# A held load, column sums moved forward and feed-forward casts put in order, in a one-core hybrid encoder layer

## The chip, the core and the metric

The kernel runs on one core of a Trainium2 chip. A core has a matrix engine (TensorE, PE in the profile, with its weight loads shown apart as PEld), a vector engine (DVE), a scalar engine (ACT), GpSimd (POOL) and SyncE (SP). Each takes its own instructions in the order in which they stand in its program. Transfers from memory are issued by SP, ACT or POOL. The metric is the time of one execution on the device in microseconds, taken as the median of several runs.

## What is computed

One layer of a streaming encoder on x (512 rows of 1024) with 256 memory rows of 1024, everything float32:

```python
u = rmsnorm(h, g_mix)
gq, gk, gv, gg, ga, fq, fk, fv, ff, mq, gates = split_cols(u @ w_in, PROJ_SIZES)
...
mk, mv = split(rmsnorm(mem, g_mem) @ w_mem_kv)
...
merged = gt[0] * y_gla + gt[1] * y_fox + gt[2] * y_mem
h = h + merged @ w_out
u2 = rmsnorm(h, g_ffn)
h = h + square(relu(u2 @ w_ff1)) @ w_ff2
return rmsnorm(h, g_final)
```

`rmsnorm` divides each row by the root of its mean square and multiplies by a gain. The three branches (gated linear attention, forgetting attention, attention into the memory rows) lie between the first projection and `merged`; the change does not touch them.

## The kernel before

A float32 product is made of three products of rounded halves: every operand is split into a high part (`hi`, a copy rounded to fp32r, mostly by ACT) and a low part (`lo`, the operand minus its high part, by DVE), and PE forms high by high, high by low and low by high. So each weight of 128x1024 values (512 KB) costs a load, one cast on ACT and one subtraction on DVE before PE can use it. Weights lie in memory as numbered chunks (`wst`). The pool `wp` has three slots each for raw weights, for `hi` and for `lo`, taken in turn: a cast waits until PE has read the weight that held its slot.

PE's program order is the order of the code. The other engines' order is set by a planner that simulates the kernel at build time, except where it is written by hand: `in_order` chains all DVE, ACT and SP instructions traced inside it in the order of the code, and `tc.issue_after(ins)` (also as `behind(ins)`) puts the instructions of its block behind `ins` if they run on the same engine as `ins`. Neither adds a wait between engines. `tc.add_manual_dep(..., Sync, ...)` does: the instruction waits until the other has ended.

The front goes so. Ten matmuls on zeros (L302) keep PE busy until data are there. The memory rows come in four pairs (`mem_load`), each 128 partitions of two times 256 values; the first carries 24 columns of gains behind it. Pairs 0 and 1 go through ACT's queue, pairs 2 and 3 through SP's. For each of eight k, ACT multiplies the rows by their gain (`mxh`, L321) and DVE makes the low part (`mxl`, L323). `lead` loads the chunks 0 to 3 (weights of the memory keys), each split in two halves by ACT (L286) and DVE (L288); chunk 0 is loaded in two halves. `mem_keys` multiplies them (L391, twelve matmuls for each k).

Chunks 4 to 7 are the weights of the memory values. `mem_values` is a generator of 16 pieces, four for each chunk: for two row tiles the products with `hi` (four matmuls each), then for both those with `lo` (two each), at L404. Chunks 4 and 5 come through `lead`, chunks 6 and 7 (the third and the fourth) into `vraws`, whose tiles are those of chunks 3 and 4, and are split by `lead_w` (L416, L417).

x arrives in quarters (`x_load`, L339). `x_square` (L344) squares each on ACT; DVE adds the squares up (`x_sum`, L350) into `ssum`. Behind x on SP stand chunk 6 (L360), the identity (L361), chunk 7 (L362), the query and key weights of the forgetting attention and a small weight `g_raw` (all L153), then constants. Column sums (L430, eight matmuls of one column) give the row sums of squares; DVE scales them (L431), POOL takes the power (L432), and four transposes with the identity spread the result over all partitions (L437). Then for each of eight k: DVE scales x (L441), ACT makes `uhi` (L444), DVE makes `ulo` (L447). Inside that loop, behind the second `uhi`, ACT casts the small weight into `gw` (L457), a `hi` slot that chunk 7 held. PE begins the first projections with `uhi` and `ulo` as they come (`first_pair`, L609, L521, L522, L618), with the last two pieces of `mem_values` in between; when these end, ACT copies their results out (L407, `gqT`).

Much later, `w_out` is multiplied in two halves of 512 columns by `gN`, four chunks each. In the first half the chunks come one after the other, 24 PE steps each, through `get_w` (slots of `wp`). In the second half (`c1`) all four are asked for at once: the first two through `own_w` into tiles of their own (`f0`, `f1`; split at L223 and L224), the last two through `get_w`, hence `split_w` (L160, L161). A row tile then takes 24 steps: six for each chunk. When 24 units of `c1` have been issued (three row tiles), the first two feed-forward weights (`f2`, `f3`) are asked for with `own_w`. Their casts and subtractions are placed by the planner. `split_w` remembers its cast and subtraction in `cast_now` and `low_now`. The feed-forward part that follows works in four quarters of the inner width.

Of the kernel before, what the change touches and what calls it, by code (L numbers as in the profile page):

```python
# [13 lines left out]
AF = mybir.ActivationFunctionType  # L14
ALU = mybir.AluOpType
AX = mybir.AxisListType

P = 128
# [45 lines left out]
def hybrid_block(ctx, tc, chunks, wst, memT, xT, xN, gffn, gfin, wup, cst, out):  # L64
# [201 lines left out]
    with pool("front") as fp:  # L266
# [6 lines left out]

        def lead(key, loads=1, parts=1, after=(None, None, None)):

# [3 lines left out]
            for i in range(loads):  # L279
                sl = slice(i * 1024 // loads, (i + 1) * 1024 // loads)  # L280
                with behind(after[0]):
                    d = nc.sync.dma_start(raw[:, sl], wst[index[key]][:, sl]).ins
            for i in range(parts):
                sl = slice(i * 1024 // parts, (i + 1) * 1024 // parts)
                with behind(after[1]):
                    a = nc.scalar.copy(hi[:, sl], raw[:, sl]).ins  # L286
                with behind(after[2]):
                    v = nc.vector.tensor_tensor(lo[:, sl], raw[:, sl], f(hi[:, sl]), op=ALU.subtract).ins  # L288
                after = yield d, a, v
# [11 lines left out]
        for _ in range(10):  # L301
            nc.tensor.matmul(ps, wz[:, :P], wz, start=True, stop=True)  # L302
        def mem_load(eng, j, end=0, after=None):
            n = 2 * M
            at = j and j * P * n + P * 24
            with behind(after):
                return eng.dma_start(mem_s[:, (3 - j) * n:(4 - j) * n + end],
                                     memT[at:at + P * (n + end)].rearrange("(p c) -> p c", p=P)).ins

        mem_load(nc.scalar, 0, 24)  # L310
        d = mem_load(nc.scalar, 1)
        with tc.issue_after(d):
            act = nc.scalar.activation(warm, warm, AF.Exp).ins
        vec, load = None, None
        for j in range(4):
            parts = None
            if j > 1:
                load = mem_load(nc.sync, j, after=load)
            for k in (2 * j, 2 * j + 1):
                with behind(act):  # L320
                    act = nc.scalar.mul(mxh[:, k, :], memr[:, KT - 1 - k, :], gmem[:, k:k + 1]).ins  # L321
                with behind(vec):
                    vec = nc.vector.scalar_tensor_tensor(mxl[:, k, :], memr[:, KT - 1 - k, :], gmem[:, k:k + 1], f(mxh[:, k, :]),  # L323
                                                         op0=ALU.mult, op1=ALU.subtract).ins
                if parts is None:
                    parts = lead(chunks[j], 1 if j else 2, 2, (load, act, vec))
                    load, act, vec = next(parts)
# [7 lines left out]
        next(lead(chunks[4], after=(load, act, vec)))  # L335
        sqs = []

# [3 lines left out]
        def x_square(j):  # L341
            sq = fp.tile([P, 2, S], F32, tag="xsq", name=nm("xsq"), bufs=3)
            for k in range(2) if j == 3 else [slice(0, 2)]:
                nc.scalar.activation(sq[:, k], xt[:, 2 * j:2 * j + 2, :][:, k], AF.Square)  # L344
            if j == 1:
# [13 lines left out]
        vraws = [fp.tile([P, 1024], F32, tag="lead", name=nm("raw"), bufs=2) for _ in range(2)]  # L359
        nc.sync.dma_start(vraws[0], wst[6])  # L360
        nc.sync.dma_start(ident, cst[:, :P])  # L361
# [63 lines left out]
        lead_w(chunks[6], vraws[0])()  # L425
        run(islice(mv, 9))
        lead_w(chunks[7], vraws[1])()
        ps = at_()
        for t in range(NT):
            nc.tensor.matmul(ps[:, t:t + 1], ssum[:, t * P:(t + 1) * P], ones[:, 0:1], start=True, stop=True)  # L430
        nc.vector.tensor_scalar(ms, ps[:, :NT], 1.0 / D, EPS, op0=ALU.mult, op1=ALU.add)  # L431
        nc.gpsimd.tensor_tensor(rx, ms, mhalf[:, :NT], op=ALU.pow)  # L432
        k_copies(range(4))
        run(islice(mv, 3))
        rb = at_()
# [29 lines left out]
        u_low(KT - 1)  # L465
        run(islice(mv, 2))
        for j in range(4):
# [562 lines left out]
    with pool("outp") as op_:  # L1030
# [219 lines left out]
        run(islice(c1, 24))  # L1250
        ws = [own_w(("F", 0, 0, b)) for b in ("11", "21")]

# [614 lines left out]
def layout(inputs):  # L1867
# [48 lines left out]
    pairs = [tl(mem)[:, 2 * j:2 * j + 2][:, ::-1].reshape(P, -1) for j in range(4)]  # L1916
    mem_flat = np.concatenate([np.concatenate([pairs[0], cols], axis=1).ravel()] + [x.ravel() for x in pairs[1:]])
    wup = np.zeros((P, 264), np.float32)
# [47 lines left out]
```

## Time and profile before

| | us |
|---|---|
| median of 3 runs | 810.16 |
| lowest, highest run | 809.69, 810.54 |
| the profiled execution | 811.06 |
| its span, first to last instruction | 809.3 |

Times inside a profile count from the start of its span. A line of the timeline has the start, the duration, the engine, the line of the program, the operation, what it writes and reads, the shape and how often; in brackets stands how long the engine was idle before it and what ended this. A line of waits has the engine and what it did, whom it waited for, the sum, the number and the longest. A line of the stretches has the stretch, its length, the busy time of PE, PEld, DVE, ACT and POOL with their instructions, the granted clock, the share of the transfer engines and GB/s. In this execution the granted clock of PE was 0.997 of full speed.

### The profile page before, as it was taken

What the parts mean: (1) busy time and instruction counts of PE and PEld (TensorE: products, weight loads), DVE (VectorE), ACT (ScalarE), POOL (GpSimd) and SP (SyncE); (2) the same over time, 40 slices, a digit from 0 to 9 for tenths busy, and PEclk for the clock granted to TensorE, in tenths of its full rate; (3) what the DMA queues carried; (4) which work ended last, traced back from release to release, by engine and by line L of the source; (5) the groups of instructions that cost most, each with busy time, mean ns of one, the idle gap of its engine ahead of it and who ended that gap; (6) DMA issues with size and microseconds to landing.
All of it is one profiled execution on the core that took longest, in us unless ns stands there. A gap on an engine that the chain in (4) does not pass through costs nothing.

```text
span 809.3 us, 12486 instructions
## 1 busy us (share of the span) xinstructions
PE 800.1 (99%) x4799; PEld 704.9 (87%) x4799; DVE 595.6 (74%) x917; ACT 444.7 (55%) x702; POOL 108.0 (13%) x136
## 2 busy tenths in 40 slices
PE   9999999999999999999999999999999999999996
PEld 7788888888888888999999879988998899889985
DVE  6878878456465677877567368897788778877897
ACT  7767555443344234444354347874676367647764
POOL 0001010101101111143144000011001100100011
PEclk9999999999999999999999999999999999999998
DMA  9355665788887867757758723898758966896544
GB/s 358 137 160 175 185 164 178 213 226 246 215 266 239 234 210 198 186 138 206 204 134 238 254 81 130 275 258 217 240 165 195 220 213 173 191 274 202 162 83 130
DMA packets 39628, 161.29 MB, mean 199 GB/s; under 512 B 4752, under 2 KB 5456, under 8 KB 37200
## 3 DMA queue, kind: packets, MB, share of 16 engines
q0 software_dynamic: 9776, 58.20, 34.3%
q1 hardware_dynamic: 28432, 98.34, 34.2%
q10 hardware_dynamic: 1360, 3.96, 1.5%
q8 instruction: 37, 0.61, 0.3%
q14 instruction: 23, 0.19, 0.1%
HBM read 158.35 MB, written 35.68 MB: 240 GB/s over the span
## 4 chain that ended last, share of the span: by engine, by line
PE 94%; DMA 2%; DVE 1%; ACT 1%; issue 0%; POOLq 0%; DVEq 0%; POOL 0%; ACTq 0%
PE mm L1272 20%; PE mm L170 16%; PE mm L171 16%; PE mm L172 16%; PE a L171 5%; PE a L170 5%; PE a L172 5%; DMA raw<-in_wst_dram 2%; PE mm L391 1%; PE a L404 1%; PE a L662 1%; PE a L700 1%; PE a L699 1%; PE a L302 1%; PE a L939 1%; PE mm L618 0%
## 5 line engine op out<-in xcount | busy, mean ns | idle before, releaser
L170 PE MATMUL mm<-uhi,whi 128*128 128x512 f32 (+1 forms) x336 | 119.7, 356 | 0.0
L161 DVE TENSOR_TENSOR wlo<-raw,whi 128x1024 fp32r<-128x1024 f32 x61 | 79.6, 1306 | 53.0 <-ACT whi L160 53.0
L172 PE MATMUL mm<-uhi,wlo 128*128 128x512 f32 (+1 forms) x336 | 117.5, 350 | 0.0
L171 PE MATMUL mm<-ulo,whi 128*128 128x512 f32 (+1 forms) x336 | 117.3, 349 | 0.0
L160 ACT CAST whi<-raw 128x1024 fp32r<-128x1024 f32 x61 | 64.1, 1052 | 84.2 <-PE mm L171 47.8
L1328 ACT CAST hi<-raw 128x1024 fp32r<-128x1024 f32 x52 | 54.4, 1049 | 41.1 <-PE mm L1272 29.5
L1330 DVE TENSOR_TENSOR lo<-raw,hi 128x1024 fp32r<-128x1024 f32 x52 | 63.4, 1223 | 15.7 <-ACT hi L1328 15.7
L170 PEld LDWEIGHTS mm<-uhi,whi 128*128 128x128 f32 x336 | 63.7, 190 | 9.3 <-issue 1.5
L172 PEld LDWEIGHTS mm<-uhi,wlo 128*128 128x128 f32 x336 | 63.6, 189 | 8.5
L171 PEld LDWEIGHTS mm<-ulo,whi 128*128 128x128 f32 x336 | 63.7, 190 | 7.5
L1272 PE MATMUL mm<-u2l,hi 128*128 128x256 f32 x240 | 66.1, 283 | 0.0
L1272 PE MATMUL mm<-u2h,hi 128*128 128x256 f32 x240 | 66.1, 283 | 0.0
L1272 PE MATMUL mm<-u2h,lo 128*128 128x256 f32 x240 | 61.1, 283 | 0.0
L1632 POOL DMA_DIRECT2D b<-in_wst_dram x30 | 25.6, 855 | 262.2 <-DVE lo L1330 136.0
L1272 PE MATMUL mm<-u2sh,hi 128*128 128x256 f32 x192 | 52.5, 283 | 0.0
L1272 PE MATMUL mm<-u2sl,hi 128*128 128x256 f32 x192 | 52.5, 283 | 0.0
L170 PE MATMUL mm<-hi,ch 128*128 128x512 f32 (+1 forms) x132 | 50.9, 386 | 0.0
L171 PE MATMUL mm<-lo,ch 128*128 128x512 f32 (+1 forms) x132 | 50.9, 386 | 0.0
L172 PE MATMUL mm<-hi,cl 128*128 128x512 f32 (+1 forms) x132 | 50.9, 386 | 0.0
L1272 PE MATMUL mm<-u2sh,lo 128*128 128x256 f32 x192 | 47.5, 283 | 0.0
L1272 PEld LDWEIGHTS mm<-u2h,hi 128*128 128x128 f32 x240 | 46.1, 192 | 0.1
L1272 PEld LDWEIGHTS mm<-u2l,hi 128*128 128x128 f32 x240 | 46.1, 192 | 0.1
(446 smaller groups left out, 2144.9 us busy)
## 6 DMA issues: line engine op xcount, KB each, us to landing
raw<-in_wst_dram SPq DMA_DIRECT2D x113, 512.0 KB
raw<-T SPq DMA_DIRECT2D x32, 512.0 KB
b<-in_wst_dram POOLq DMA_DIRECT2D x32, 512.0 KB, 5.5
T<-in_wst_dram POOLq DMA_DIRECT2D x12, 1024.0 KB, 9.0
b<-in_wst_dram SPq DMA_DIRECT2D x16, 512.0 KB
wb<-in_wst_dram POOLq DMA_DIRECT2D x15, 512.0 KB, 5.4
T<-in_wst_dram POOLq DMA_DIRECT2D x12, 512.0 KB, 6.0
wb<-in_wst_dram SPq DMA_DIRECT2D x8, 512.0 KB
```

The costliest lines, as they stand in the source:

```text
L160: cast = nc.scalar.copy(hi, raw)
L161: low_now[0] = nc.vector.tensor_tensor(lo, raw, f(hi), op=ALU.subtract).ins
L170: nc.tensor.matmul(ps, lh, rh, start=start, stop=False, skip_group_check=on)
L171: nc.tensor.matmul(ps, lh, rl, start=False, stop=False, skip_group_check=on)
L172: nc.tensor.matmul(ps, ll, rh, start=False, stop=stop, skip_group_check=on)
L302: nc.tensor.matmul(ps, wz[:, :P], wz, start=True, stop=True)
L391: nc.tensor.matmul(kps[h], w[:, h * P:(h + 1) * P], x[:, k, :], start=k == p == 0, stop=k == KT - 1 and p == 2)
L404: nc.tensor.matmul(ps, x[:, k, sl], w[low][:, kk, :], start=k == low == 0 and x is mxh, stop=k == KT - 1 and low == 1)
L1272: nc.tensor.matmul(ps[:, a, :], x[:, a, k, :], y[:, s, k, :], start=start, stop=stop, skip_group_check=go is not None)
L1328: nc.scalar.copy(hi, raw)
L1330: nc.vector.tensor_tensor(lo, raw, f(hi), op=ALU.subtract)
L1632: nc.gpsimd.dma_start(to[i], wst[index["B", q, i, x]], accum_op=ALU.add)
```

## The change

There are four edits.

The start: the first pair of memory rows is loaded in two pieces on ACT's queue, with the gains in the first, and pair 1 moves to SP's queue, between the first and the second weight chunk. The high part of the first half of chunk 0 is made by DVE with a copy (`head=True`), ahead of DVE's first `mxl`, not by ACT.

The held load: the load of chunk 6 waits, as a dependency between engines, for the square of x's second quarter (`squares[1]`).

The column sums: they stand behind six pieces of `mem_values` instead of nine. Four pieces (before: three) come between them and the transposes, four (before: two) behind the transposes, and two are left for `first_pair` as before. So the sums stand three pieces and the transposes two pieces further forward. The low part of chunk 7 is traced behind the power and waits for it.

The feed-forward weights: the casts and subtractions of `f2` and `f3` are put behind the cast and the subtraction of the last chunk of `w_out`.

```diff
--- before.py
+++ after.py
@@ -271,7 +271,7 @@
         xt = fp.tile([P, KT, S], F32, name="xt")
         pre = {}
 
-        def lead(key, loads=1, parts=1, after=(None, None, None)):
+        def lead(key, loads=1, parts=1, after=(None, None, None), head=False):
 
             late = index[key] in (3, 4)
             raw = (fp if late else wp).tile([P, 1024], F32, tag="lead" if late else "raw", name=nm("raw"), bufs=2 if late else 3)
@@ -280,10 +280,15 @@
                 sl = slice(i * 1024 // loads, (i + 1) * 1024 // loads)
                 with behind(after[0]):
                     d = nc.sync.dma_start(raw[:, sl], wst[index[key]][:, sl]).ins
+            if head:
+                sl = slice(0, 1024 // parts)
+                after = yield d, None, nc.vector.tensor_copy(hi[:, sl], raw[:, sl]).ins
             for i in range(parts):
                 sl = slice(i * 1024 // parts, (i + 1) * 1024 // parts)
-                with behind(after[1]):
-                    a = nc.scalar.copy(hi[:, sl], raw[:, sl]).ins
+                a = after[1]
+                with behind(a):
+                    if i or not head:
+                        a = nc.scalar.copy(hi[:, sl], raw[:, sl]).ins
                 with behind(after[2]):
                     v = nc.vector.tensor_tensor(lo[:, sl], raw[:, sl], f(hi[:, sl]), op=ALU.subtract).ins
                 after = yield d, a, v
@@ -300,21 +305,24 @@
         ps = at_()
         for _ in range(10):
             nc.tensor.matmul(ps, wz[:, :P], wz, start=True, stop=True)
-        def mem_load(eng, j, end=0, after=None):
+        def mem_load(eng, j, after=None, cols=None):
             n = 2 * M
-            at = j and j * P * n + P * 24
+            a, b = cols or ((3 - j) * n, (4 - j) * n)
+            at = (KT * M + 24 - b) * P
             with behind(after):
-                return eng.dma_start(mem_s[:, (3 - j) * n:(4 - j) * n + end],
-                                     memT[at:at + P * (n + end)].rearrange("(p c) -> p c", p=P)).ins
-
-        mem_load(nc.scalar, 0, 24)
-        d = mem_load(nc.scalar, 1)
+                return eng.dma_start(mem_s[:, a:b], memT[at:at + P * (b - a)].rearrange("(p c) -> p c", p=P)).ins
+
+        mem_load(nc.scalar, 0, cols=(7 * M, 8 * M + 24))
+        d = mem_load(nc.scalar, 0, cols=(6 * M, 7 * M))
         with tc.issue_after(d):
             act = nc.scalar.activation(warm, warm, AF.Exp).ins
         vec, load = None, None
         for j in range(4):
             parts = None
-            if j > 1:
+            if j == 0:
+                parts = lead(chunks[0], 2, 2, head=True)
+                load, _, vec = next(parts)
+            if j:
                 load = mem_load(nc.sync, j, after=load)
             for k in (2 * j, 2 * j + 1):
                 with behind(act):
@@ -322,8 +330,10 @@
                 with behind(vec):
                     vec = nc.vector.scalar_tensor_tensor(mxl[:, k, :], memr[:, KT - 1 - k, :], gmem[:, k:k + 1], f(mxh[:, k, :]),
                                                          op0=ALU.mult, op1=ALU.subtract).ins
-                if parts is None:
-                    parts = lead(chunks[j], 1 if j else 2, 2, (load, act, vec))
+                if k == 0:
+                    load, act, vec = parts.send((load, act, vec))
+                elif parts is None:
+                    parts = lead(chunks[j], 1, 2, (load, act, vec))
                     load, act, vec = next(parts)
                 else:
                     _, act, vec = parts.send((None, act, vec))
@@ -333,7 +343,11 @@
         order = in_order()
         order.__enter__()
         next(lead(chunks[4], after=(load, act, vec)))
-        sqs = []
+        sqs, squares = [], []
+
+        def behind_of(ins, other):
+            tc.add_manual_dep(ins, other.name, mybir.DependencyInfo(mybir.DependencyClass.Sync, mybir.DependencyReason.DATA),
+                              reason="pace")
 
         def x_load(j):
             nc.sync.dma_start(xt[:, 2 * j:2 * j + 2, :].rearrange("p k t -> p (k t)"), xT[j])
@@ -341,7 +355,7 @@
         def x_square(j):
             sq = fp.tile([P, 2, S], F32, tag="xsq", name=nm("xsq"), bufs=3)
             for k in range(2) if j == 3 else [slice(0, 2)]:
-                nc.scalar.activation(sq[:, k], xt[:, 2 * j:2 * j + 2, :][:, k], AF.Square)
+                squares.append(nc.scalar.activation(sq[:, k], xt[:, 2 * j:2 * j + 2, :][:, k], AF.Square).ins)
             if j == 1:
                 nc.vector.tensor_tensor(sq, sq, sqs[0], op=ALU.add)
             sqs.append(sq)
@@ -357,7 +371,7 @@
         for j in range(2, 4):
             x_load(j)
         vraws = [fp.tile([P, 1024], F32, tag="lead", name=nm("raw"), bufs=2) for _ in range(2)]
-        nc.sync.dma_start(vraws[0], wst[6])
+        behind_of(nc.sync.dma_start(vraws[0], wst[6]).ins, squares[1])
         nc.sync.dma_start(ident, cst[:, :P])
         nc.sync.dma_start(vraws[1], wst[7])
         fraws = [load_w(("T", "w_in", OFF[n])) for n in ("fq", "fk")]
@@ -423,15 +437,16 @@
         ms, rx = (small(fp, NT, g) for g in ("ms", "rx"))
         mv = mem_values()
         lead_w(chunks[6], vraws[0])()
-        run(islice(mv, 9))
-        lead_w(chunks[7], vraws[1])()
+        run(islice(mv, 6))
+        low = lead_w(chunks[7], vraws[1])
         ps = at_()
         for t in range(NT):
             nc.tensor.matmul(ps[:, t:t + 1], ssum[:, t * P:(t + 1) * P], ones[:, 0:1], start=True, stop=True)
         nc.vector.tensor_scalar(ms, ps[:, :NT], 1.0 / D, EPS, op0=ALU.mult, op1=ALU.add)
-        nc.gpsimd.tensor_tensor(rx, ms, mhalf[:, :NT], op=ALU.pow)
+        power = nc.gpsimd.tensor_tensor(rx, ms, mhalf[:, :NT], op=ALU.pow).ins
+        behind_of(low().ins, power)
         k_copies(range(4))
-        run(islice(mv, 3))
+        run(islice(mv, 4))
         rb = at_()
         for t in range(NT):
             nc.tensor.transpose(rb[:, t * P:(t + 1) * P], rx[:, t:t + 1].to_broadcast([P, P]), ident)
@@ -463,7 +478,7 @@
             if k == 5:
                 nc.vector.tensor_tensor(wup_s[32:64], wup_raw[32:64], f(wup_s[32:64]), op=ALU.subtract)
         u_low(KT - 1)
-        run(islice(mv, 2))
+        run(islice(mv, 4))
         for j in range(4):
             nc.scalar.activation(msq[j], mem_s[:, 2 * M * j:2 * M * (j + 1)], AF.Square)
         for op in lows:
@@ -1248,7 +1263,8 @@
         run(gN([("N", "w_out", 2 * j, 0) for j in range(4)], of(mh, ml), NT, at_, res_evac(0)))
         c1 = gN([("N", "w_out", 2 * j, 512) for j in range(4)], of(mh, ml), NT, mmt, res_evac(1), tail=4, get=out_w)
         run(islice(c1, 24))
-        ws = [own_w(("F", 0, 0, b)) for b in ("11", "21")]
+        with tc.issue_after(cast_now[0]), tc.issue_after(low_now[0]):
+            ws = [own_w(("F", 0, 0, b)) for b in ("11", "21")]
 
         def u2_turn(t):
             for g in range(2):
@@ -1914,7 +1930,8 @@
     cols[:, 16:20] = np.asarray(inputs["g_gla_head"])[0].T
     cols[24, 20] = cols[56, 20] = 1.0
     pairs = [tl(mem)[:, 2 * j:2 * j + 2][:, ::-1].reshape(P, -1) for j in range(4)]
-    mem_flat = np.concatenate([np.concatenate([pairs[0], cols], axis=1).ravel()] + [x.ravel() for x in pairs[1:]])
+    first = np.concatenate([pairs[0][:, M:], cols], axis=1)
+    mem_flat = np.concatenate([x.ravel() for x in [first, pairs[0][:, :M]] + pairs[1:]])
     wup = np.zeros((P, 264), np.float32)
     wup[0:16, 0:256] = np.asarray(inputs["w_alpha_up"])[0]
     wup[16:24, 256:264] = np.eye(8, dtype=np.float32)
```

## The prediction

> **What bounds the kernel now.** I read the page's busy times first, then busy time by stretch, then what TensorE (PE) and its weight loads (PEld) waited for.
>
> ```profile
> span 809.3 us, 12486 instructions
> ...
> PE 800.1 (99%) x4799; PEld 704.9 (87%) x4799; DVE 595.6 (74%) x917; ACT 444.7 (55%) x702; POOL 108.0 (13%) x136
> ```
>
> ```profile
> 45.00:230.00 185.00, 184.97 (x959) 154.72 (x958) 122.95 (x298) 95.99 (x208) 16.40 (x23) 1.00 0.70 202
> 230.00:437.00 207.00, 207.00 (x1348) 185.32 (x1347) 142.17 (x196) 87.28 (x122) 48.24 (x51) 1.00 0.74 201
> ...
> 495.00:802.00 307.00, 307.00 (x1973) 281.17 (x1973) 258.49 (x317) 200.64 (x272) 29.22 (x38) 1.00 0.73 199
> ```
>
> ```profile
> PE mm L171 <- DVE wlo L161: 1.0, 1, 1.0
> ```
>
> ```profile
> PEld mm L609 <- DVE ulo L447: 1.2, 3, 0.5
> ```
>
> The second column of a stretch is its length, the third PE's busy time. PE is full in all three long stretches, so other engines matter only where they make PE wait. Two such places are left that the change touches: one wait of 1.0 us on the low half of a weight (`wlo`), and three in the front, 1.2 us together, on the low half of the normalised x (`ulo`). The first matmul is a third place. No PE instruction is removed, so the change can win little more than these waits.
>
> **Part 1: feed-forward weights behind.** The one long wait, then ACT, DVE and SP around it:
>
> ```profile
> 465.83 0.39 PE L170 MATMUL mm<-whi,mh 128*128 128x512 f32 x1
> 467.21 0.50 PE L171 MATMUL mm<-wlo,mh 128*128 128x512 f32 x1 [0.99 <-DVE wlo L161]
> 467.55 0.39 PE L172 MATMUL mm<-whi,ml 128*128 128x512 f32 x1
> 467.78 0.39 PE L170 MATMUL mm<-whi,mh 128*128 128x512 f32 x1
> ```
>
> ```profile
> 452.49 1.05 ACT L160 CAST whi<-raw 128x1024 fp32r<-128x1024 f32 x1 [2.58 <-DMA raw<-in_wst_dram]
> 460.43 1.05 ACT L223 CAST f2h<-raw 128x1024 fp32r<-128x1024 f32 x1 [6.88 <-DMA raw<-in_wst_dram]
> 463.12 1.05 ACT L223 CAST f3h<-raw 128x1024 fp32r<-128x1024 f32 x1 [1.64 <-DMA raw<-in_wst_dram]
> 464.08 1.04 ACT L160 CAST whi<-raw 128x1024 fp32r<-128x1024 f32 x1
> ```
>
> ```profile
> 465.94 1.22 DVE L161 TENSOR_TENSOR wlo<-raw,whi 128x1024 fp32r<-128x1024 f32 x1
> ```
>
> ```profile
> 449.29 2.60 SPq L153 DMA_DIRECT2D raw<-in_wst_dram  x3
> ```
>
> `f2h` and `f3h` are the first two feed-forward weights; the two `whi` are the third and fourth `w_out` weights of the second half. The fourth is cast last, behind two feed-forward casts that each waited for their load. Its own load was among the three issued from 449.29 on, as was the third's, which had landed by 452.49; so its data were probably there some 11 us before 464.08. With the edit both feed-forward casts stand behind that cast and both their lows behind its low. The fourth then needs only its slot in the ring of three, which the third weight of the first half holds. PE left that one 42 steps before 465.83 (24 with the fourth weight, 18 of the second half), at 0.23 us each 9.7 us, or at 456.2. Cast and low take 1.04 and 1.22 and are over by 459.
>
> The price: three PE steps from 465.83 to the same operation at 467.78 took 1.95 us; at the 0.23 us between 467.55 and 467.78 they take 0.68. The edit gains **1.27 us**. Bounds: 0, if something else there is as late as 467.21, and 1.27. I take 1.27: between 437 and 480 us PE shows no second wait. The feed-forward casts themselves wait for loads that land at 460.43 and 463.12, later than a fourth `w_out` cast needs, so nothing of theirs moves. Their SP loads get no new order, because the new order binds instructions of the same engine only.
>
> **Part 2: the start.** The new head lets DVE make the first half of the first weight's high part, and splits the first memory load.
>
> ```profile
> 1.19 4.45 PE L302 MATMUL a<-wz 128*128 128x512 bf16 x10 [1.19 <-DVE warm L299]
> ...
> 5.00 0.48 DVE L323 SCALAR_TENSOR_TENSOR mxl<-mem_s,mxh 128x256 fp32r<-128x256 f32 x1 [3.86 <-ACT mxh L321]
> ...
> 5.53 0.91 PE L391 MATMUL mm<-mxh,hi 128*128 128x256 f32 x4
> ...
> 7.09 0.62 ACT L286 CAST hi<-raw 128x512 fp32r<-128x512 f32 x1 [0.28 <-DMA raw<-in_wst_dram]
> ...
> 8.56 0.55 PEld L391 LDWEIGHTS mm<-mxh,hi 128*128 128x128 f32 x4
> ```
>
> The ten warm-up matmuls stay and end at 5.64, so an earlier operand can hardly start PE earlier than 5.53: gain 0 to 0.1 us. The new copy on DVE, 512 columns, has no row; between 0 and the 0.65 us that a two-input operation of that size takes (27.25 in part 4, two in 1.29), I take 0.65, the nearest kind. It falls into DVE's 3.86 idle us; without that cover it would push the operation at 5.00 to an end at 6.13, and PE's first four matmuls last to 6.44. ACT loses one cast of 0.62. The second pair of memory rows goes from ACT's queue to SP's, ahead of the second weight, whose cast began at 7.09. If that costs a 256 KB transfer, half of the 1.31 us between the two landings quoted in part 3, or 0.65, the cast ends at 8.36, still before the 8.56 at which PE wants it. What PE gains here it gives back in part 4, where x sets the time. I take 0.
>
> **Part 3: the held load.**
>
> ```profile
> 13.46 0.33 SPq L360 DMA_DIRECT2D raw<-in_wst_dram  x1
> ```
>
> ```profile
> 14.84 1.06 ACT L344 ACTIVATE xsq<-xt 128x1024 f32<-128x1024 f32 x1 [0.21 <-DMA xt<-in_xT_dram]
> ...
> 20.04 1.16 ACT L344 ACTIVATE xsq<-xt 128x512 f32<-128x512 f32 x2 [1.59 <-DMA xt<-in_xT_dram]
> ...
> 21.35 1.05 ACT L416 CAST hi<-raw 128x1024 fp32r<-128x1024 f32 x1 [0.15 <-DMA raw<-in_wst_dram]
> ```
>
> The load leaves SP at 13.46; it will wait for the second square, which ends at 15.90, and behind it on SP stand the identity, the fourth values' weight, both query/key weights, the small weight and the constants. It lands at 21.35, 7.9 us after its issue, right behind x's fourth quarter (20.04): transfers queue. Issued at 15.95 it still has 5.4 us to get where it was. Gain from it: between 0 and 1.31 us for x's fourth quarter, if the two shared the engines evenly. Loss: between 0 and the full 2.45 us on everything behind it. I take 0, for the 5.4 us.
>
> The Trainium skill, "DMA: Bandwidth & Descriptors", section "Queues, rings and completion order", says that each DMA engine consumes one ring's descriptors in order. By it a load queued behind x cannot have slowed x, and this edit is worth nothing, as taken; the sum by sharing would be up to 0.9 us better (second rival).
>
> **Part 4: the column sums.**
>
> ```profile
> 20.71 1.49 DVE L350 TENSOR_TENSOR xsq<-xsq,xsq 128x512 f32<-128x512 f32 x2 [0.36 <-ACT xsq L344]
> ```
>
> ```profile
> 21.76 0.89 PEld L404 LDWEIGHTS a<-lo,mxh 128*128 128x128 f32 x4
> ...
> 23.64 1.09 PEld L430 LDWEIGHTS a<-ones,xsq 128*128 128x128 f32 x8
> ...
> 24.64 0.19 PEld L404 LDWEIGHTS a<-hi,mxh 128*128 128x128 f32 x1
> ...
> 25.31 1.03 POOL L432 TENSOR_TENSOR rx<-ms,mhalf 128x4 f32<-128x4 f32 x1 [20.62 <-DMA raw<-in_wst_dram]
> ...
> 26.39 0.58 PEld L437 LDWEIGHTS a<-cst_s,rx 128*128 128x128 f32 x4
> ```
>
> ```profile
> 27.25 1.29 DVE L441 TENSOR_TENSOR xt<-xt,a 128x512 f32<-128x512 f32 x2 [2.09 <-PE a L437]
> ```
>
> With six pieces ahead instead of nine PE reaches the sums at 21.76. Their input ends at 22.20, so PE waits about 0.49, a new wait, and starts at 22.25. The sums take 1.00 (23.64 to 24.64), ending at 23.25; then come four pieces, 1.88 for three (21.76 to 23.64) and about 0.85 for the other, less what overlaps: the broadcast starts at about 25.95 instead of 26.39. POOL's power, 1.67 behind the sums before (25.31), ends at 24.95, in time; the fourth low, held behind it, takes 1.22 and ends at 26.2, before x's first scaling at 26.8 (27.25 less 0.44). So DVE gains 0.44 there. But ACT has an order of its own:
>
> ```profile
> 28.69 0.39 PE L404 MATMUL a<-hi,mxl 128*128 128x512 f32 x1
> ```
>
> ```profile
> 29.28 1.04 ACT L457 CAST whi<-raw 128x1024 fp32r<-128x1024 f32 x1
> ...
> 30.22 0.57 ACT L407 COPY gqT<-a 128x512 f32<-128x512 f32 x1
> ...
> 30.69 0.72 ACT L444 ACTIVATE uhi<-xt,cols_s 128x512 fp32r<-128x512 f32 x1
> ```
>
> The small weight's cast (29.28) goes into the slot of the fourth values' weight, so it waits for the last piece that reads this: 28.69 plus 0.39, or 29.08. That piece keeps its place behind the same work, so PE's new wait moves its end to 29.57 and the cast to 29.6, 0.32 later; the third `uhi` is ordered behind it. At 30.22 a copy of the memory values slipped in between. If it stays there, the third `uhi` moves from 30.69 to 31.0 and the front loses about 0.35. If it goes behind, `uhi` starts at 30.55 and the front gains 0.14. I take the second, since x is scaled earlier and ready first; PE's `ulo` waits shrink, but PE still ends on them. **Front: -0.14**, bounds -0.9 (x early) and +1.4 (third rival).
>
> **The sum.** -1.27 - 0.14 = -1.41. The profiled execution took 811.06 (its span of 809.3 and 1.8 around it), so 809.65 by it; the median of the runs is 810.16, 0.90 lower, and 1.41 off that is 808.75. I say **808.8**.
>
> **The rivals.**
>
> Second: x's fourth quarter does land earlier because the held load no longer shares with it. Then PE meets the sums at 21.76 without the wait, the small weight's cast keeps 29.28 or less, and the front gains 0.5 to 0.9: 808.0 to 808.4. For it: the 1.31 us between the landings is the price of one such load. Against: the load was queued behind x.
>
> Third: the hold passes on in full. Everything behind it lands 2.45 later, the query/key casts end behind `uhi`'s start, and ACT, which had about 1.1 us to spare, delays the front by 1.4: 810.16 - 1.27 + 1.4 = 810.3, a hair slower than before. For it: SP works in order. Against: the 5.4 us.
>
> Fourth, slower: outside the front a planner with simulated times orders ACT, DVE, POOL and SP. Starting times shift, and it may put casts in a worse order in the feed-forward loop, as it did at 464.08. That loop runs four times; one such swap at 1.27 us in each of them is 5.1 us, against 1.4 won: 813.9. Two quarters hit lose 1.1 net, from the third on it passes 811.8. Against: 307.00 us busy of 307, and PE has no wait there to start from.
>
> **Chances.** First 0.45 (808.3 to 809.3, where the copy's order moves it), second 0.23, third and mixtures with it 0.16, fourth 0.16. The measurement tells about 0.2%, or 1.6 us, from no change. Faster than 808.5 are the second and a fifth of the first: 0.32. Slower than 811.8 is the fourth, nearly whole: 0.15. The same: 0.53. The range reaches from 807.7, a little under the second's end, to 811.8, past the third.
>
> **What would show it.** Right: no `wlo` wait near 466, the fourth `w_out` cast ahead of both feed-forward casts; a new wait of about 0.5 us at the column sums, x's last squares still at 20.0; the small weight's cast at 29.6; less `ulo` waiting. Wrong: squares at 19 (second rival), query/key casts after 27 (third), any PE wait after 45 us (fourth), or a wait near 466 that only changes its name.

## The result and the profile after

| | before | after |
|---|---|---|
| median, us | 810.51 (22 runs, 809.63 to 813.95) | 812.13 (22 runs, 810.78 to 815.2) |
| ratio to before | | 1.0016, 95% interval 1.0008 to 1.0023 |
| profiled execution; its span | 811.06; 809.3 | 812.61; 810.8 |
| first matmul of the memory keys | 5.53 | 5.16 |
| first projection begins (first weight load of L170) | 45.62 | 48.37 |
| from there to the end of the span | 763.7 | 762.5 |

The change costs 1.6 us where the forecast was a gain of 1.4. The last two rows split it: the front is 2.75 us longer, everything behind it 1.2 shorter. Behind the front stands the feed-forward edit. Busy time between 437 and 480 us, then ACT's casts, both of the kernel after (lines have moved: L170 to L172, L160, L223 stayed, L430 became L444, L344 L358, L404 L418, L286 L291, L350 L364):

```profile
437.00:480.00 43.00, 43.00 (x203) 36.08 (x202) 25.45 (x35) 17.34 (x27) 11.68 (x12) 1.00 0.70 203
```

```profile
462.13 1.05 ACT L160 CAST whi<-raw 128x1024 fp32r<-128x1024 f32 x1 [5.78 <-DMA raw<-in_wst_dram]
463.31 1.06 ACT L223 CAST f2h<-raw 128x1024 fp32r<-128x1024 f32 x1
464.70 1.06 ACT L223 CAST f3h<-raw 128x1024 fp32r<-128x1024 f32 x1 [0.33 <-DMA raw<-in_wst_dram]
```

PE is busy for all of the 43 us (42.01 before), and the fourth `w_out` cast now stands ahead of `f2h` and `f3h`. The front is the other half. First what its weight loads waited for between 19 and 46 us, then the timeline of PE, and busy time in short stretches (the third column from the right is the granted clock):

```profile
PEld a L444 <- issue: 2.3, 1, 2.3
PEld mm L624 <- DVE ulo L462: 0.4, 1, 0.4
```

```profile
21.38 0.40 PE L418 MATMUL a<-hi,mxl 128*128 128x512 f32 x1
23.69 1.02 PE L444 MATMUL a<-ones,xsq 128*128 128x1 f32 x8 [1.91 <-DVE xsq L364]
24.57 1.80 PE L418 MATMUL a<-lo,mxh 128*128 128x512 f32 x4
26.17 0.63 PE L418 MATMUL a<-hi,mxh 128*128 128x512 f32 x1
26.59 0.63 PE L418 MATMUL a<-hi,mxl 128*128 128x512 f32 x1
...
28.54 0.40 PE L418 MATMUL a<-hi,mxh 128*128 128x512 f32 x1
28.77 0.40 PE L418 MATMUL a<-hi,mxl 128*128 128x512 f32 x1
```

```profile
24.00:24.50 0.50, 0.50 (x7) 0.50 (x6) 0.50 (x1) 0.50 (x2) 0.00 (x0) 1.00 0.97 393
24.50:25.00 0.50, 0.50 (x4) 0.46 (x5) 0.34 (x2) 0.50 (x3) 0.00 (x0) 0.87 0.99 410
25.00:26.00 1.00, 1.00 (x4) 0.81 (x3) 0.00 (x0) 1.00 (x4) 0.94 (x1) 0.50 1.03 410
26.00:27.00 1.00, 1.00 (x3) 0.73 (x3) 0.88 (x1) 0.50 (x1) 0.09 (x1) 0.50 0.74 260
27.00:28.00 1.00, 1.00 (x4) 0.78 (x3) 0.34 (x1) 0.00 (x0) 0.00 (x0) 0.50 0.21 71
28.00:28.50 0.50, 0.50 (x3) 0.39 (x2) 0.00 (x0) 0.00 (x0) 0.00 (x0) 0.71 0.00 1
28.50:29.00 0.50, 0.50 (x3) 0.32 (x2) 0.00 (x0) 0.00 (x0) 0.00 (x0) 1.00 0.00 0
```

Two costs stand here. The column sums start 2.33 us late (the weight loads' idle time ahead of them). And from about 24.9 to 28.3 the granted clock is 0.50, with a pitch of 0.42 between matmuls (26.17, 26.59) and not 0.23 (28.54, 28.77): 3.4 us of work at half speed, 1.7 lost. With the start 0.37 earlier and 0.8 less waiting for `ulo` (0.4, before 1.2) that makes +2.9; measured is +2.75. A busy share cannot show the second cost: PE counts as busy at either clock.

The late input, on ACT and DVE of the kernel after:

```profile
18.31 1.05 ACT L291 CAST hi<-raw 128x1024 fp32r<-128x1024 f32 x1 [1.99 <-DVE xsq L364]
19.35 1.07 ACT L358 ACTIVATE xsq<-xt 128x1024 f32<-128x1024 f32 x1
20.69 1.16 ACT L358 ACTIVATE xsq<-xt 128x512 f32<-128x512 f32 x2 [0.27 <-DVE lo L293]
```

```profile
21.25 2.29 DVE L364 TENSOR_TENSOR xsq<-xsq,xsq 128x512 f32<-128x512 f32 x3
```

The sum is complete at 23.54; before it was at 22.20. The first sign is the cast of chunk 5, at 18.31 instead of 16.2, and ACT was idle 1.99 us ahead of it. The releaser that the row names, a sum of squares on DVE, is none: in most other executions this cast ran at 16.2 to 16.8, ahead of that sum. It is the weight's own load that was late, as the landings listed with `e6_fetch` show. x itself was late as well: its third and fourth quarter landed at 19.33 and 20.61 and were squared at once, at 19.35 and 20.69, so the late cast held nothing up.

### The profile page after: what moved, and what is told of

Same layout as the page of the kernel before. It is cut to its first block, busy times and chain, and to the rows that moved or that the text cites. A ratio compares the mean times of both kernels' runs of the same rounds, so it can differ in the third digit from the quotient of the medians.

```text
span 810.8 us, 12489 instructions
## 1 busy us (share of the span) xinstructions
PE 800.7 (99%) x4799; PEld 706.1 (87%) x4799; DVE 596.0 (74%) x918; ACT 445.4 (55%) x701; POOL 108.0 (13%) x136
## 4 chain that ended last, share of the span: by engine, by line
PE 96%; DMA 2%; DVE 1%; ACT 0%; issue 0%; SPq 0%; POOLq 0%; DVEq 0%; ACTq 0%; POOL 0%
PE mm L1288 20%; PE mm L170 17%; PE mm L171 16%; PE mm L172 16%; PE a L171 6%; PE a L170 6%; PE a L172 6%; DMA xt<-in_xT_dram 1%; PE a L418 1%; PE mm L624 1%; PE a L677 1%; PE a L715 1%; PE a L714 1%; DMA mem_s<-in_memT_dram 1%; PE a L954 1%; PE mm L633 0%
## 5 line engine op out<-in xcount | busy, mean ns | idle before, releaser
L170 PE MATMUL mm<-uhi,whi 128*128 128x512 f32 (+1 forms) x336 | 119.7, 356 | 0.0
L172 PE MATMUL mm<-uhi,wlo 128*128 128x512 f32 (+1 forms) x336 | 117.5, 350 | 0.0
L160 ACT CAST whi<-raw 128x1024 fp32r<-128x1024 f32 x61 | 64.2, 1053 | 89.5 <-PE mm L171 47.7
L170 PEld LDWEIGHTS mm<-uhi,whi 128*128 128x128 f32 x336 | 63.7, 190 | 9.3 <-issue 1.4
L172 PEld LDWEIGHTS mm<-uhi,wlo 128*128 128x128 f32 x336 | 63.6, 189 | 8.5
L170 PE MATMUL mm<-hi,ch 128*128 128x512 f32 (+1 forms) x132 | 50.9, 386 | 0.0
L172 PE MATMUL mm<-hi,cl 128*128 128x512 f32 (+1 forms) x132 | 50.9, 386 | 0.0
```

The lines of the kernel that those rows point to most:

```text
L160: cast = nc.scalar.copy(hi, raw)
L170: nc.tensor.matmul(ps, lh, rh, start=start, stop=False, skip_group_check=on)
L172: nc.tensor.matmul(ps, ll, rh, start=False, stop=stop, skip_group_check=on)
```

## The experiments

**Feed-forward edit alone** (`e1_ff_only`):

```diff
-        ws = [own_w(("F", 0, 0, b)) for b in ("11", "21")]
+        with tc.issue_after(cast_now[0]), tc.issue_after(low_now[0]):
+            ws = [own_w(("F", 0, 0, b)) for b in ("11", "21")]
```

> The kernel before with the fourth edit alone (feed-forward casts behind). Theory A (the loss is all in the front: PE meets column sums whose input is 1.35 us late, waits 2.3 us and then runs at half clock): no wait on a low half near 466, the front as before (first matmul of the first projection at 45.6), about 1.3 us less than before: 809.2 beside 810.5. Rival B (the order behind costs something later, in the feed-forward quarters): the wait near 466 gone, but 810.2 to 812.

Measured: 810.3 beside 810.63, ratio 0.9994 (0.9985 to 1.0002). In the trace there is no wait near 466, the first projection begins at 45.66, and 762.6 us pass from there to the end: 1.1 less than before, near the 1.3 expected. The medians show only 0.3 of it, and 810.3 lies in the range of rival B, though no later wait of PE is to be seen. Why the medians gain less than the traces is open; the second profile of before, below, bears on it.

**The held load taken out, the column sums put back, the old start put back** (each from the kernel after):

```diff
-        behind_of(nc.sync.dma_start(vraws[0], wst[6]).ins, squares[1])
+        nc.sync.dma_start(vraws[0], wst[6])
```

> The kernel after without the held load. Theory A, with the late input blamed on the start and not on the hold: x's last squares still near 20.7, the wait at the column sums still about 2.3 us, the half clock stays, 812 beside the 812.1 of the kernel after. Rival C (the hold, by what it does to the queues, is what makes x late): squares back at 20.0, the wait at 0.5 or below, no half clock, 808.8 to 809.5. Rival D (x's fourth quarter would be later still without the hold): a longer wait, 812.5 to 813.5.

```diff
-        run(islice(mv, 6))
-        low = lead_w(chunks[7], vraws[1])
+        run(islice(mv, 9))
+        lead_w(chunks[7], vraws[1])()
...
-        behind_of(low().ins, power)
         k_copies(range(4))
-        run(islice(mv, 4))
+        run(islice(mv, 3))
```

> The kernel after with the column sums and the transposes where they were (9, 3 and 2 pieces; the low part of chunk 7 without its wait). Theory A: x's input is as late as in the kernel after (sums of squares ready near 23.5), but PE has three pieces more to do and gets to the column sums near 23.3, waits 0.3 or less, keeps its full clock; the front is as in the kernel before, 809.0 to 809.5. Rival: if the late input itself, not the place of the sums, sets the end of the front, the first projection stays 2 us later and the time stays at 811 to 812.

For `e4_old_start`, `lead`, `mem_load`, the loop over j and the layout of the memory rows are those of before.

> The kernel after with the start as it was (memory pairs 0 and 1 on ACT's queue, the first half weight cast by ACT). Theory E (the new start moves PE and its instruction fetch 0.4 to 0.8 us ahead, so that the fetch holds up chunk 5 and x behind it): chunk 5 is cast near 16.2, x's last squares are at 20.0, PE reaches the column sums at 21.8 and waits about 0.5 us, no half clock, 808.6 to 809.3. Rival C (the hold makes x late): last squares at 20.7 or later, a wait over 1 us, 810.5 to 812.

| kernel | median (ratio, interval) | wait at the sums | clock 0.50 behind it | first projection |
|---|---|---|---|---|
| `e2_no_hold` | 811.61 (1.0011, 1.0002 to 1.0020) | 2.27 | yes | 48.48 |
| `e3_sums_back` | 810.55 (0.9999, 0.9990 to 1.0007) | 0 | no | 46.38 |
| `e4_old_start` | 811.16 (1.0007, 0.9996 to 1.0019) | 1.42 | yes | 47.79 |

The hold is not the cause: without it the front looks the same. With the sums behind nine pieces the wait and the half clock are gone although x is as late (last squares at 20.68). Its first projection still comes 0.8 later than before's, and 810.55 misses the expected 809.0 to 809.5. The old start shortens the wait, to 1.42 and not to the expected 0.5, and the clock still drops; 811.16 misses the expected 808.6 to 809.3. Its chunk 5 came in time (cast at 16.21), but x's third quarter did not:

```profile
16.21 1.05 ACT L286 CAST hi<-raw 128x1024 fp32r<-128x1024 f32 x1 [0.28 <-DMA raw<-in_wst_dram]
18.86 1.06 ACT L348 ACTIVATE xsq<-xt 128x1024 f32<-128x1024 f32 x1 [1.60 <-DMA xt<-in_xT_dram]
20.26 1.16 ACT L348 ACTIVATE xsq<-xt 128x512 f32<-128x512 f32 x2 [0.34 <-DMA xt<-in_xT_dram]
```

That square ran at 17.38 in the trace of before. So with one and the same start another transfer can be the late one.

**What makes a transfer late** (`e6_fetch`, from the kernel before):

```diff
-        for _ in range(10):
-            nc.tensor.matmul(ps, wz[:, :P], wz, start=True, stop=True)
+        for n in [512] * 8 + [1] * 16:
+            nc.tensor.matmul(ps[:, :n], wz[:, :P], wz[:, :n], start=True, stop=True)
```

> The kernel before with 8 instead of 10 matmuls on zeros, and 16 more of one column behind them: 14 more matmuls and weight loads, 28 instructions of PE, which at some 17 per us are 1.6 us of its program. Theory H (the 16 KB instruction fetch is PE's own, at a fixed place of its program): the fetch starts near 15.1, not 16.7, and holds up x's second quarter or chunk 5 on one engine, so that its cast or square comes 1.3 us late. Rival: the fetch is another engine's and stays at 16.6 to 16.8.

The transfers of the kernel after from 16.0 to 16.6 by queue (packets, MB, share of 16 engines), then those of this kernel from 15 to 16; each has one packet of a queue of its own:

```profile
q1 hardware_dynamic: 59, 0.23, 96.9%
q8 instruction: 1, 0.02, 11.2%
```

```profile
q1 hardware_dynamic: 109, 0.39, 96.0%
q8 instruction: 1, 0.02, 6.8%
```

From the raw records of the transfers and their landings, in us (a load is spread over 16 engines; landing on the 15th, then on the last of them):

```
kernel         fetch (16 KB)  chunk 5         x third quarter  x fourth quarter
before         16.80, 1.08    16.00  16.10    17.27  17.36     18.63  19.96
e4_old_start   16.62, 1.03    16.07  16.11    17.40  18.84     18.65  20.18
e6_fetch       15.12, 1.08    16.32  17.60    17.57  18.89     18.86  20.17
after          16.04, 1.08    16.47  18.21    17.73  19.33     19.00  20.61
r2_after       16.85, 1.03    16.45  16.45    17.72  19.06     18.98  20.22
```

Each execution has one fetch of instructions in this time, 16,384 bytes in about 1.05 us on one transfer engine. The transfer that comes next on that engine lands 1.2 to 1.7 us after the other fifteen, and so does everything behind it, for all engines are full: in the kernel after the stretch from 15 to 20 us has a share of 1.02 and 391 GB/s,

```profile
15.00:20.00 5.00, 5.00 (x32) 4.40 (x31) 2.77 (x4) 2.80 (x4) 0.00 (x0) 1.00 1.02 391
```

and no engine can catch up. One trace is milder: in `e11_all_sums8` the next load was 0.6 late, its engines being further apart already.

With 28 instructions more ahead of it on PE the fetch moved from 16.8 to 15.1, as forecast from PE's rate of some 17 a us: it is PE's own. All 14 traces bear this out: the fetch starts when PE has begun 199 to 209 matmuls and weight loads (203 in `e6_fetch` at 15.12, 203 in `e11_all_sums8` at 17.02). The late transfer moved with it, from x to chunk 5, whose cast ran at 17.70:

```profile
17.70 1.05 ACT L286 CAST hi<-raw 128x1024 fp32r<-128x1024 f32 x1 [1.57 <-PE mm L391]
```

In the trace of the kernel after PE was early enough for the fetch to meet chunk 5, with both quarters of x behind it. The Trainium skill, "Runtime: NRT & Kernel Launch", section "Instruction fetch mechanics", has instructions come in blocks of 16 KiB over a queue of the sequencer's own, the cost "mostly hidden"; size and queue agree with the records. For PE it is hidden here, for the loads behind it it is not.

**PE kept busy during the wait** (`e5_fill`, from the kernel after):

```diff
         ps = at_()
+        for _ in range(10):
+            nc.tensor.matmul(ps, wz[:, :P], wz, start=True, stop=True)
         for t in range(NT):
```

> The kernel after with ten more matmuls on zeros (about 2.2 us at full clock) between the six pieces and the column sums; their result is overwritten, the output is the same. Theory A (PE's idle time at the column sums drops the clock): the granted clock from 24 to 29 is 1.00, the matmul pitch there 0.23 and not 0.43, the first projection starts 1.5 to 1.8 us earlier than in the kernel after (46.6 to 46.9 beside 48.37), and the runs lose their upper end: 810.3 to 811.3 in the median. Rival G (the clock drops for another reason, such as the load on the chip at that moment): half clock again, 812 to 814.

The trace answers the question. The sums' input was as late as in the kernel after (their weight loads began at 23.69, there at 23.66), and the clock stayed at 1.00 in each stretch:

```profile
25.00:26.00 1.00, 1.00 (x6) 0.78 (x5) 0.06 (x1) 1.00 (x4) 0.79 (x1) 1.00 0.99 392
26.00:27.00 1.00, 1.00 (x6) 0.81 (x5) 0.73 (x1) 0.50 (x1) 0.23 (x1) 1.00 0.74 262
27.00:28.00 1.00, 1.00 (x9) 0.81 (x7) 0.49 (x1) 0.18 (x1) 0.00 (x0) 1.00 0.19 64
```

The first projection begins at 46.98 instead of 48.37: the idle PE is what drops the clock, and in these two traces that is worth 1.4 us. The time went the other way and missed the expected range: 813.93, 1.0040 (1.0026 to 1.0054), over 5 runs. Two waits in the feed-forward part of the trace are 1.15 of it:

```profile
543.17 0.50 PE L171 MATMUL a<-lo,ch 128*128 128x512 f32 x1 [0.45 <-DVE lo L1405]
549.65 0.50 PE L171 MATMUL mm<-lo,ch 128*128 128x512 f32 x1 [0.70 <-DVE lo L1348]
```

DVE, ACT, POOL and SP have exactly the order of the kernel after there, whose trace shows neither wait; `e4_old_start` shows both, at 0.5 and 0.7, and `e6_fetch`, without the feed-forward edit, has one of 0.43 at 548. Another part lies outside the span: the five runs took 1.8 to 2.9 us more than their spans, all runs of the other kernels 1.7 to 1.8. What makes those low halves late in some executions, and what else this kernel loses, was not found.

**Second profiles of both kernels** (no edit):

> The kernel before once more, for a second profile of it. Theory F (the wait of 0.99 us near 466 is not in every execution: with the fourth edit alone the shortest runs are no shorter than before's shortest): no wait on a low half near 466, span below 809. Rival: the same wait again, within 0.2 us. In either case x's third or fourth quarter is held up on one engine by an instruction fetch that starts at 16.6 to 16.8.

> The kernel after once more, for a second profile of it. Theory A (how late x is depends on which transfer the instruction fetch meets, so the wait and the clock drop vary from one execution to the next): a wait at the column sums between 1 and 2.5 us; with half clock behind it the first projection at 48 or later, without at 46 to 46.7. Rival: always the same 2.3 us and half clock.

The second trace of before has the wait near 466 again, shorter:

```profile
467.60 0.50 PE L171 MATMUL mm<-wlo,mh 128*128 128x512 f32 x1 [0.61 <-DVE wlo L161]
```

Its span is 809.6, so that expectation failed; with 0.99 and, in `e6_fetch`, 0.35, the wait is in all three traces that lack the fourth edit, and the one that the forecast was made on has the longest. The time from the first projection to the end is 763.7 or 763.8 in all three, however long the wait, so this wait alone does not account for it. The fetch came at 16.90 and met x's fourth quarter. The second trace of the kernel after, weight loads and vector adds:

```profile
23.31 0.97 PEld L444 LDWEIGHTS a<-ones,xsq 128*128 128x128 f32 x8 [1.21 <-issue]
```

```profile
20.91 2.29 DVE L364 TENSOR_TENSOR xsq<-xsq,xsq 128x512 f32<-128x512 f32 x3
```

```profile
24.00:26.00 2.00, 2.00 (x12) 1.68 (x12) 0.72 (x3) 2.00 (x6) 1.03 (x1) 1.00 1.01 386
26.00:28.00 2.00, 2.00 (x12) 1.66 (x11) 1.24 (x2) 0.73 (x2) 0.00 (x0) 1.00 0.27 93
```

Here the clock rose to full only at 7.12 us, not at 4.39, and PE was 0.8 us behind from there on. The fetch came at 16.85 and met x's third quarter, the sums were complete at 23.20, PE reached them at 22.10 and waited 1.21, and the clock stayed up. The first projection began at 46.47 and the span was 808.9, against 48.37 and 810.8. So the kernel after has both courses.

Its 22 runs bear this out. A stretch of 3.4 us at half clock lowers the mean granted clock of a run by 0.002. Seven runs have 0.993 to 0.996; they took 812.16 to 815.2, median 812.42. The other 15 took 810.78 to 813.42, median 811.30. The two kernels that also have the sums behind six pieces, `e2_no_hold` and `e4_old_start`, have four and two such runs of 12; none of the 67 runs of the six kernels with eight or nine pieces and the feed-forward edit is below 0.997. Seven is the least, since the profiled run of `e4_old_start` has the half clock and 0.997. The other 15, some of which may have it too, are still 0.8 above before in the median.

**One part alone, or one part less.** `e10_start_ff` is before with the new start and the feed-forward edit; `e8_sums8` is before with the feed-forward edit and the sums one piece forward; `e12_hold_sums8` adds the hold to that; `e11_all_sums8` is the kernel after with eight pieces instead of six. For the last three:

```diff
-        run(islice(mv, 6))
+        run(islice(mv, 8))
         low = lead_w(chunks[7], vraws[1])
...
         k_copies(range(4))
-        run(islice(mv, 4))
+        run(islice(mv, 3))
...
         u_low(KT - 1)
-        run(islice(mv, 4))
+        run(islice(mv, 3))
```

> The kernel before with the new start and the fourth edit; no held load, column sums behind nine pieces as before. Theory A (the start alone puts x's data about 0.3 us later and PE 0.5 us earlier): x's last squares near 20.7, the column sums at 24.0 to 24.2 with a wait of at most 0.3, full clock, the first projection at 46.2 to 46.4 as with the held load, 810.3 to 810.8. Rival C (the held load leaves the transfer engines idle for a while near 20 to 22 and that delays the last values' weight): without it the first projection starts at 45.6 to 45.8, 809.8 to 810.2.

> The kernel before with the fourth edit and the column sums one piece forward (8, 3 and 3 pieces; the low part of chunk 7 behind the power), the start and the load of chunk 6 as before. Theory A: PE gets to the column sums near 23.4, when their input (22.2 to 23.0) is there: no wait over 0.3, full clock; the transposes are about 0.45 earlier, the waits on the low half of x shrink from 1.2 to 0.8, the first projection starts at 45.2 to 45.4; 0.3 to 0.5 us less than with the fourth edit alone: 809.8 to 810.1. Rival: another wait (query and key casts, the small weight's cast) takes the 0.45 back, 810.3 to 810.8.

> The best kernel so far (old start, column sums behind eight pieces, fourth edit) with the held load added. Theory A (the hold is worth nothing either way): the load leaves SP near 16.0 and not 13.6, x's last squares stay at 20.1 to 20.3, transfers stay near 400 GB/s from 18 to 25, the first projection at 45.3 to 45.5, 809.6 to 810.1 beside 809.8. Rival C: x later or transfers with a gap, 0.5 us or more slower, 810.3 or above; or, if the hold helps x, squares at 19.5 and 809.3 or below.

> The kernel after with the column sums behind eight pieces instead of six (8, 3 and 3); start, held load and feed-forward order as in the kernel after. Theory A: PE gets there near 22.8 and the input is ready at 23.5: a wait of 0.6 to 0.9 instead of 2.3, no or little half clock; the first projection at 45.8 to 46.4 beside 48.37; 810.0 to 810.8. Rival: any idle time of PE there drops the clock, and the first projection comes at 47 or later, 811 to 812.

| kernel | start | hold | pieces ahead | median (ratio, interval) | wait at the sums | first projection |
|---|---|---|---|---|---|---|
| `e1_ff_only` | old | no | 9 | 810.30 (0.9994, 0.9985 to 1.0002) | 0 | 45.66 |
| `e10_start_ff` | new | no | 9 | 810.71 (0.9999, 0.9991 to 1.0008) | 0 | 45.84 |
| `e8_sums8` | old | no | 8 | 809.79 (0.9985, 0.9976 to 0.9994) | 0.4 | 45.39 |
| `e12_hold_sums8` | old | yes | 8 | 810.01 (0.9994, 0.9985 to 1.0002) | 0.5 | 45.42 |
| `e11_all_sums8` | new | yes | 8 | 810.19 (0.9993, 0.9984 to 1.0002) | 0.4 | 45.65 |
| after | new | yes | 6 | 812.13 (1.0016, 1.0008 to 1.0023) | 1.2 and 2.3 | 46.47 and 48.37 |

In the first five rows the granted clock is 1.00 from 20 to 45 us. The last two rows differ in nothing but the place of the sums and the transposes: two pieces cost 1.9 us. In the traces eight pieces bring the first projection 0.2 to 0.3 earlier than nine with the same start and without the hold, and the waits for `ulo` shrink; the intervals of the medians of `e8_sums8` and `e1_ff_only` overlap, so the gain of eight over nine is not shown. These are the waits of the weight loads in `e8_sums8` from 19 to 46 us, all of them:

```profile
PEld mm L614 <- DVE ulo L452: 0.4, 1, 0.4
PEld a L434 <- issue: 0.4, 1, 0.4
```

In `e1_ff_only` there are three for `ulo` with 1.2 us together. `e8_sums8` is the one kernel whose interval lies below 1: it is faster than before, by 1.0 us beside the 810.79 that before took on the same chip, and so than the kernel after. That is 0.15% by the ratio, less than the bound of 0.2% that the prediction set, but the interval excludes no change. Of the expectations, those of `e8_sums8` (but for a wait of 0.39, where 0.3 was the most expected) and `e12_hold_sums8` held; `e11_all_sums8` kept its time, with a shorter wait than expected; `e10_start_ff` kept its time too, but its first projection was 0.4 earlier than theory A said.

## Why the prediction was wrong

**The step that failed** is in part 4: "Their input ends at 22.20, so PE waits about 0.49". The mechanism was named, and its size was wrong: 2.33 us in one trace and 1.21 in the other, 4.8 and 2.5 times the forecast. Both ends of the subtraction were taken from one execution of before. The input's end ranges from 22.20 to 23.66 in the traces, and 22.20 is the earliest of them. It depends on which load PE's instruction fetch meets: with the old start it is 22.20 and 22.36 where this is x's fourth quarter, 22.95 to 23.09 in the five other traces. The new start adds to it: 23.17 to 23.66 in all seven. And PE got there at 21.33 in one trace, 22.10 in the other, not at 21.76. The small weight's cast, the term behind it, came at 32.49 and 30.61 instead of 29.6. Nine pieces had hidden all of this: before's sums began at 23.64, 1.4 us after their input.

**The clock was not in the sum at all.** The working priced a wait at its length. Behind waits of 1.42, 2.27 and 2.33 PE's clock fell to half for 3.4 us, which adds 1.7 by its length and 1.4 by the comparison with `e5_fill`, which shows that it is the idle time that does it. Without the drop the front of the second trace is 0.85 longer than before's, so the forecast of -0.14 fails by the wait alone too.

**Part 2** took 0 for the start, since PE could "hardly start" earlier than 5.53. It started at 5.16: the end of the warm-up at 5.64 was no bound, since without work queued right behind it, as in `e1_ff_only` with the same start, it ends at 5.03 (5.76, where the first of the keys' matmuls starts, less 0.73 idle). By itself the start is worth about 0.2 us to the bad (first projection 45.66 to 45.84 with nine pieces, 45.42 to 45.65 with eight); both differences are of single traces. It frees PE earlier, where the clock rises early, and delivers x later.

**Part 3** took 0 for the held load, and that held within what the runs tell: first projections at 45.39 and 45.42 without and with it, 48.48 and 48.37 in the kernel after, medians 0.2 and 0.5 higher with it, and 0.2 lower in `e3_sums_back` than in `e10_start_ff`. x's last squares came at 20.14 and 20.18 without and with it, at 20.89 and 20.69 in the kernel after, at 20.42 and 20.68 with nine pieces: no steady gain and nothing near 19, so the second rival falls. The rule of the Trainium skill on the order within a ring ("DMA: Bandwidth & Descriptors", "Queues, rings and completion order") would have it so. Nor did a delay pass on in full (third rival). There is a small debt with the new start and nine pieces: without the hold transfers ran at 406 GB/s from 20 to 22 us (`e10_start_ff`), with it at 280 (`e3_sums_back`), chunk 7's cast came at 23.73 instead of 23.18, and the first projection at 46.38 instead of 45.84. The second of the query and key casts did come after 27 in the kernel after (29.20, and 27.32 in its second trace), which was to show the third rival; it waited for PE to free a slot, not for a load.

**Part 1** was right in kind. Behind the front the nine traces with the edit and without the feed-forward waits have 762.3 to 763.0 us to the end, the three without the edit 763.7: 1.1 on average against 1.27. That leaves out two traces with the edit that have these waits, `e4_old_start` and `e5_fill`, at 764.4 and 764.1. And 1.27 is what the longest of three observed waits gave, and the medians show 0.3 (interval 1.2 less to 0.2 more). One argument for it was false: the fourth weight's load was not there 11 us early. In `e1_ff_only` it landed just ahead of its cast at 459.08, late enough for an idle ACT:

```profile
459.08 1.05 ACT L160 CAST whi<-raw 128x1024 fp32r<-128x1024 f32 x1 [5.30 <-DMA raw<-in_wst_dram]
```

Cast and low still end by 461.4 there and by 464.5 in the kernel after, and PE wants them near 466.

**The fourth rival**, the planner putting the feed-forward loop in a worse order, was the only one on the slower side of 811.8, for a reason that did not occur: behind 480 us DVE, ACT, POOL and SP have the same order in the traces of before and after, and PE is full from 495 to 802 in the latter. Nor did the range of Part 4's term help: the front moved by +2.75 and +0.85, and its upper end (+1.4) came from a passed-on hold and not from the wait itself.

## What to carry to other kernels

Before a consumer is moved forward towards its input, take the input's arrival from several executions and keep the latest; a margin of 1.4 us that looks idle in one trace may be what absorbs the spread. Price a new wait on the matrix engine with the clock: here waits of 1.42 us and more cost 1.4 to 1.7 again, in matmuls that count as busy, and one of 1.21 did not. A gain read off one execution's wait is not yet the gain of the median: three traces of it had 0.99, 0.61 and 0.35.

## What was not expected of the hardware

PE's fetches of its own program pass through the same transfer engines as the loads, as the landings above show. Where these are full (a share of 1.02), one fetch of 16 KB made every following load 1.2 to 1.7 us late on one of sixteen engines (0.6 in one trace), and a load is complete with its last engine. Adding 28 PE instructions in the warm-up changed which tensor is hit.

The half clock came after idle times of 2.33, 2.27 and 1.42 us, each with about a microsecond of one-column matmuls behind it, and not after 1.21. Length alone need not be what decides. By the raw records of the clock, the times between its changes are whole multiples of 3.413 us in all 14 traces: in the kernel after it rose at 4.39, fell at 24.87 (six steps) and rose again at 28.29 (one step). Where these steps lie differs between executions: the first rise came at 4.28 to 7.12. In the step in which the column sums began, matmuls of 512 columns were busy for 0.61, 0.67 and 1.52 us in the three traces whose clock then fell (`after`, `e2_no_hold`, `e4_old_start`), for 1.76 in `r2_after` and for 2.4 or more in the others, whose clock stayed up. What exactly is counted, and where between 1.52 and 1.76 the bound lies, if it is one, no run here separates.

The Trainium skill, "TensorE: Matmul & The Clock Gate", "Part 1: The HAM clock gate (the "warmup" mystery)", explains such drops by a free-running window of about 3.4 us that must be idle. The steps and the length of the slow phase fit that; a window that is idle throughout does not, since in `e4_old_start` PE was idle for 1.42 us of it and, even with the one-column matmuls taken as idle, for 2.4.
